# Attention of a decoder step: lone tokens in two parts by halves of the heads, one scaling of four on GpSimd, new cache rows written in a step of their own

## The chip, the cores and the metric

The kernel runs on one core of a Trainium2 chip. The core has a matrix engine (TensorE, PE in the profile; its weight loads are PEld), VectorE (DVE), ScalarE (ACT), GpSimd (POOL) and SyncE (SP), which here issues most transfers. The metric is the time of one execution on the device in microseconds (us), lower is better; "before" is the median of three runs.

## The reference, cut to what matters

One inference step of a two-layer decoder, for a prompt of 512 tokens and for 8 samples of one new token each. The change lies in the attention of the second layer. There are 16 query heads of 64 numbers in 4 groups of keys and values; each head has a sink, a logit that only enters the denominator.

```python
q = _rope((h @ w_q[j]).reshape(B, T, N_KV_HEADS, GROUP, HEAD_DIM), pos)
out = _window_attention(q, kk, vv, wb, pos0, attn_sinks[j]) @ w_o[j]
...
s = jnp.einsum('bnqkgd,bnskd->bnkgqs', q, k) * (HEAD_DIM ** -0.5)
s = jnp.where(mask[None, :, None, None], s, -jnp.inf)
m = jnp.maximum(jnp.max(s, axis=-1, keepdims=True), sink)
p = jnp.exp(s - m)
denom = jnp.sum(p, axis=-1, keepdims=True) + jnp.exp(sink - m)
return jnp.einsum('bnkgqs,bnskd->bnqkgd', p / denom, v)
```

For the prompt each block of 128 queries sees its own block and the one before it. Each of the 8 lone tokens sees 128 keys: 127 rows of its cache and its own new row.

## The kernel before, in words

Prompt and samples are columns of the same tiles: 520 columns, 512 of the prompt and 8 lone tokens. Every weight block is split into a high part (ScalarE, wh) and a low part (VectorE, wl), and a product is three matmuls (L513: high by high, high by low, low by high).

The attention stage is a list of named steps (class Steps). Each has an engine, a cost in us, a due time, the steps it must follow, and the buffers it takes and reads. A planner in the kernel plays this list through: whenever an engine is free it takes the step with the earliest due time whose predecessors are done. The resulting order is written out, engine by engine, and the engines run it in order. Costs and due times thus set only the order.

The steps are:

- q: eight query tiles t = 0 to 7, each of two heads e, two halves of 24 matmuls (L513, bank pa); then a copy, the rotation, a split, and the lone tokens' columns into the tile qz (L1188).
- 16 units t.h (tile t, half h of the prompt: two of four blocks). A unit is scores (L1203, bank pb, one buffer), four reductions on VectorE (L1220: mask and minimum, with the result in the tile sm), four exponents on ScalarE (L1238), two reciprocals, four scalings by them (L1246), two times transposes (L1254, bank pc) and copies (L1259), the product with the values (L1269), and the split of its result (L1280, L1284). Each row of sm has one column more, the sink's, which GpSimd writes (L1218) at a reduction's place; the exponent's sum takes it in. Of the scalings i = 0 to 3, numbers 0 and 2 are on VectorE, 1 and 3 on GpSimd.
- the lone tokens: scores with the cached keys kc (L1357), maximum with the sink, exponent, scaling, a transpose of the probabilities prS (L1396), a load of the cached values vc (L1368, on SP) with the new rows written into its first row by GpSimd (L1369), the product (L1408), a copy to oS (L1417) and a split into the columns that the projection reads (L1422, L1424). All heads of all samples go at once, due with unit 6.0; scores need all eight qz.
- o: the output projection, for each output tile m = 0 to 7 and each half g of the heads two column halves of 12 matmuls (L513). The first column half needs only the units of its four tiles; the second holds the lone tokens' columns too.

The cached keys are loaded and transposed before the stage, in the feed-forward part ahead of it: four loads (L1042), the new rows by GpSimd (L1043), transposes (L1052). The tiles kc and vc have four buffers together (tag S).

Of the kernel before, what the change touches and what calls it, by code (L numbers as in the profile page):

```python
# [231 lines left out]
class Steps:  # L232
# [15 lines left out]
    def order(self):  # L248
# [4 lines left out]
        while left:  # L253
# [13 lines left out]
            for n in left:  # L267
# [7 lines left out]
                for t in takes:  # L275
                    k = len(got[t]) - self.slots[t]
                    ok = ok and (k < 0 or all([passed(r, eng) for r in self.readers[t, got[t][k]]]))
# [21 lines left out]
def yoco_step(ctx, tc, ins, outs):  # L299
# [432 lines left out]
    with ff_pool() as tmp:  # L732
# [9 lines left out]
        sink_s = cp.tile([P, 4], F32, name="sink_s")  # L742
# [184 lines left out]
    with ff_pool() as tmp:  # L927
# [9 lines left out]
        for b in range(16):  # L937
            later(nc.sync.dma_start(sink_s[b * 8 : (b + 1) * 8, 0:2], attn_sinks.rearrange("l (g r) -> r (l g)", g=2)))
# [25 lines left out]
    with ff_pool() as tmp:  # L964
# [5 lines left out]
        V.tensor_scalar(sink_s[:, 2:4], sink_s[:, 0:2], -1.0, None, op0=ALU.mult)  # L970
        V.tensor_copy(sink_s[:, 0:2], sink_s[:, 2:4])
# [65 lines left out]
        def attention_prep():  # L1037


            for i in range(4):  # L1040
                kc.append(splp.tile([P, 2, 256], F32, tag="S", name="kc", bufs=4))
                later(nc.sync.dma_start(kc[i], cache_k[2 * i : 2 * i + 2].rearrange("b s g d -> s b (g d)")))  # L1042
                nc.gpsimd.dma_start(kc[i][0:1], knew[2 * i : 2 * i + 2, :])  # L1043
            yield
            for i in range(2):
                kk.append(pair(("tl", "tl"), [P, SP]))
                split(kk[i], kT[i][:, :SP])
                yield
            for i in range(4):
                pk = ps()  # L1050
                for j in range(4):
                    T.transpose(pk[:, j * P : (j + 1) * P], kc[i][:, j // 2, (j % 2) * P : (j % 2 + 1) * P], ident)  # L1052
                S.copy(kc[i].rearrange("p b c -> p (b c)"), pk)
                yield
# [9 lines left out]
    with tc.tile_pool(name="at", bufs=2) as at, tc.tile_pool(  # L1064
# [32 lines left out]
        o_due = lambda m, g: (u_due(9) + 14 + m * UP) if g == 0 else (u_due(16) + 4 + m * 2.87)  # L1097
        st = Steps(dict(a=2, b=1, c=2, w=6, rp=1, sm=6, pp=4))
# [105 lines left out]

        def least(t, h, i):
# [6 lines left out]
            if e == 0:  # L1212
                if (2 * t + h) % 3 < 2:
                    sm = at.tile([P, 2, 257], F32, tag="sm", name="sm", bufs=4)
                else:
                    sm = kvp.tile([P, 2, 257], F32, tag="kT", name="sm", bufs=2)
                vals["sm", t, h, bi] = sm
                nc.gpsimd.tensor_copy(sm[:, :, n], nsinks[:, 2 * t : 2 * t + 2])  # L1218
# [25 lines left out]
        def scale(t, h, i, eng):  # L1244
            w, den = part(t, h, i), vals["den", t, h]
            eng.tensor_scalar(w, w, den[:, i : i + 1], None, op0=ALU.mult)  # L1246
# [39 lines left out]
        for t in range(KT):  # L1286
            d = q_due(t)
            for h in range(2):
                add(
                    f"q{t}.{h}", "PE", 2.87, d + 3 * h, lambda t=t, h=h: q_part(t, h),  # L1290
# [11 lines left out]
            for h in range(2):  # L1302
# [4 lines left out]
                add("sc" + u, "PE", 0.9, d, lambda t=t, h=h: scores(t, h), after=chain("sc", f"ql{t}"), takes=("b",))  # L1307
                for i in range(4):
# [4 lines left out]
                        after=["sc" + u, "nw"] + ([f"rd{u}.{i - 1}"] if i else [f"rd{before}.3"] if n else []),  # L1313
                        takes=() if i % 2 else ("sm",), reads=[("b", "sc" + u)],
# [5 lines left out]
                for bi in range(2):  # L1320
# [5 lines left out]
                    for e in range(2):  # L1326
                        i = 2 * bi + e
                        eng, cost = ((nc.gpsimd, 0.5) if e else (V, 0.35))
                        add(
                            f"no{u}.{i}", "POOL" if e else "DVE", cost - 0.1 * small, d + 1.6 + 0.1 * i,  # L1330
# [5 lines left out]
                        takes=("c", "pp"), reads=[("sm", f"rd{u}.{2 * bi}")],  # L1336
# [12 lines left out]
        vc, sam = [], {}  # L1349
        s_due = u_due(12)  # L1350

        def s_scores():
            sam["ps"] = ps_ = bank()
            for c in range(4):
                for bq in range(4):
                    b, g = 4 * (c // 2) + bq, c % 2
                    T.matmul(  # L1357
                        ps_[32 * bq : 32 * bq + 32, c * P : (c + 1) * P],
                        qz[:, g, b - bq : b - bq + 4].rearrange("p b e i -> p (b e i)"),
                        kc[b // 2][:, b % 2, g * P : (g + 1) * P],  # L1360
# [4 lines left out]
        def s_values_load():  # L1365
            for i in range(4):
                vc.append(splp.tile([P, 2, 256], F32, tag="S", name="vc", bufs=4))
                later(nc.sync.dma_start(vc[i], cache_v[2 * i : 2 * i + 2].rearrange("b s g d -> s b (g d)")))  # L1368
                nc.gpsimd.dma_start(vc[i][0:1], vnew[2 * i : 2 * i + 2, :])  # L1369

        def s_max():
            sam["m"] = m = at.tile([P, 12], F32, name="smx", bufs=1)
            V.tensor_reduce(m[:, 0:4], sam["ps"].rearrange("p (c k) -> p c k", c=4), axis=AX.X, op=ALU.max)
            V.scalar_tensor_tensor(m[:, 0:4], m[:, 0:4], -1.0, sink_s, op0=ALU.mult, op1=ALU.min)
            V.tensor_tensor(m[:, 8:12], m[:, 0:4], sink_s, op=ALU.subtract)

        def s_exp():
            m = sam["m"]
            sam["pr"] = pr = big.tile([P, 512], F32, tag="tl", name="prS")
            for c in range(4):  # L1380
                cs_ = slice(c * P, (c + 1) * P)
                S.activation(pr[:, cs_], sam["ps"][:, cs_], AF.Exp, bias=m[:, c : c + 1], accum_out=m[:, 4 + c : 5 + c])
            S.activation(m[:, 8:12], m[:, 8:12], AF.Exp)

        def s_scale():
            m, pr = sam["m"], sam["pr"]
            V.tensor_tensor(m[:, 4:8], m[:, 4:8], m[:, 8:12], op=ALU.add)
            V.reciprocal(m[:, 4:8], m[:, 4:8])
            for c in range(4):
                cs_ = slice(c * P, (c + 1) * P)  # L1390
                V.tensor_scalar(pr[:, cs_], pr[:, cs_], m[:, 4 + c : 5 + c], None, op0=ALU.mult)

        def s_turn():
            sam["pt"] = pt = bank()
            for c in range(4):
                T.transpose(pt[:, c * P : (c + 1) * P], sam["pr"][:, c * P : (c + 1) * P], ident)  # L1396

        def s_turned():
            sam["prT"] = prT = big.tile([P, 512], F32, tag="tl", name="prT")
            S.copy(prT, sam["pt"])  # L1400

        def s_values():
            sam["po"] = po = bank()
            for b in range(NS):
                for g in range(2):
                    for e in range(2):
                        c0 = (2 * (b // 4) + g) * P + (b % 4) * 40 + e * 4
                        T.matmul(  # L1408
                            po[e * 64 : e * 64 + 64, b * 8 + g * 4 : b * 8 + g * 4 + 4],
                            vc[b // 2][:, b % 2, g * P + e * 64 : g * P + e * 64 + 64],  # L1410
                            sam["prT"][:, c0 : c0 + 4],
                            start=True,
                            stop=True,
                        )

        def s_out():
            V.tensor_copy(oS, sam["po"][:, :64].rearrange("p (b t) -> p t b", b=NS))  # L1417
# [165 lines left out]
```

## Time and profile before

| what | value |
|---|---|
| median of 3 runs | 1699.41 us (1698.33 to 1701.63) |
| profiled execution | 1699.45 us, span 1697.7 us |
| granted TensorE clock, mean | 0.985 |
| busy, share of the span | PE 97%, DVE 74%, ACT 52%, POOL 11% |
| attention stage, first query product to last projection matmul | 1153.55 to 1314.69 us |

The span is counted from the first to the last instruction. A row of a timeline gives the start, the duration, the engine, the line, the operation, what it writes and reads, and in brackets how long the engine had idled and what ended that. Rows of the view by stretches give the busy time of each engine with the number of its instructions, then the granted clock (1.00 is full speed) and the share of time in which the DMA engines worked.

### The profile page before, as it was taken

Reading aid. Unit: us, or ns where it says so; the run is one execution under the profiler, and the core shown is the slowest. Engines: PE = TensorE matmul, PEld = TensorE weight load, DVE = VectorE, ACT = ScalarE, POOL = GpSimd, SP = SyncE. Lnnn points to the kernel's source line nnn. Section 1 sums busy time; section 2 is a strip of 40 time slices with the busy share of each in tenths; the row PEclk is TensorE's granted clock in tenths of the full one; section 3 lists DMA queues with packets and bytes.
Section 4 is the critical chain, followed back from the end, with each engine's and each line's share of the span. In section 5 each row is a group of like instructions: output and inputs, shape, how many; then the busy total and the mean of one; then the engine's idle time right before and its main releaser. Section 6 shows DMA issues by size and latency. Waiting matters only on the chain.

```text
span 1697.7 us, 34520 instructions
## 1 busy us (share of the span) xinstructions
PE 1648.6 (97%) x13783; PEld 1630.4 (96%) x13783; DVE 1254.9 (74%) x2389; ACT 879.2 (52%) x1737; POOL 189.5 (11%) x245
## 2 busy tenths in 40 slices
PE   7999999999999999999999999999979999999996
PEld 6999999999899999999999999999869999999996
DVE  6875866887884885878775875888966785785765
ACT  6643643666552652655652652656754662562553
POOL 0101101000101101100201101102430110110100
PEclk9999999999999999999999999999979999999998
DMA  7646846663455655633755755652223566666631
GB/s 201 143 131 138 183 128 142 176 168 112 96 159 131 162 156 131 149 116 96 177 149 131 169 148 131 150 169 57 51 51 104 108 151 161 137 155 160 134 87 51
DMA packets 316145, 227.08 MB, mean 134 GB/s; under 512 B 9537, under 2 KB 291241, under 8 KB 315943
## 3 DMA queue, kind: packets, MB, share of 16 engines
q1 hardware_dynamic: 288176, 176.91, 37.0%
q0 software_dynamic: 23296, 41.82, 15.3%
q10 hardware_dynamic: 4510, 6.13, 1.2%
q8 instruction: 108, 1.77, 0.4%
q14 instruction: 55, 0.44, 0.1%
HBM read 180.89 MB, written 5.04 MB: 110 GB/s over the span
## 4 chain that ended last, share of the span: by engine, by line
PE 93%; DVE 3%; ACT 1%; DMA 1%; issue 1%; POOL 0%; SPq 0%; ACTq 0%; DVEq 0%; POOLq 0%
PE ps L538 47%; PE ps L513 36%; PE pa L513 5%; PE pb L1203 1%; PE ps L851 1%; PE ps L876 1%; DVE wl L193 1%; PE pc L1254 1%; PE pc L1269 1%; DVE sm L1220 0%; PE ps L477 0%; DMA raw<-in_ffn_w_gate_dram 0%; DVE acc L466 0%; DMA xt<-in_x_prompt_dram 0%; DMA vc<-in_cache_v_win_dram 0%
## 5 line engine op out<-in xcount | busy, mean ns | idle before, releaser
L192 ACT ACTIVATE wh<-raw 128x512 fp32r<-128x512 f32 (+1 forms) x710 | 429.7, 621 | 519.5 <-PE ps L513 297.8
L193 DVE TENSOR_TENSOR wl<-raw,wh 128x512 fp32r<-128x512 f32 (+1 forms) x710 | 469.0, 676 | 205.0 <-ACT wh L192 201.0
L538 PE MATMUL ps<-th,wh 128*128 128x260 f32 x1264 | 359.1, 284 | 1.6 <-ACT th L341 1.0
L538 PE MATMUL ps<-tl,wh 128*128 128x260 f32 x1264 | 359.7, 285 | 0.4 <-DVE tl L342 0.4
L538 PE MATMUL ps<-th,wl 128*128 128x260 f32 x1264 | 357.4, 284 | 1.0 <-DVE wl L193 1.0
L538 PEld LDWEIGHTS ps<-th,wh 128*128 128x128 f32 x1264 | 239.6, 190 | 2.6 <-ACT th L341 1.5
L538 PEld LDWEIGHTS ps<-tl,wh 128*128 128x128 f32 x1264 | 240.0, 190 | 0.8 <-DVE tl L342 0.8
L538 PEld LDWEIGHTS ps<-th,wl 128*128 128x128 f32 x1264 | 239.2, 190 | 1.5 <-DVE wl L193 1.5
L513 PE MATMUL ps<-hh,wh 128*128 128x260 f32 x1120 | 227.1, 284 | 0.6 <-ACT vtok L1027 0.6
L513 PE MATMUL ps<-hl,wh 128*128 128x260 f32 x1120 | 227.3, 283 | 0.0
L513 PE MATMUL ps<-hh,wl 128*128 128x260 f32 x1120 | 225.2, 283 | 0.0
L157 POOL DMA_DIRECT2D raw<-raw x79 | 68.9, 872 | 1264.5 <-DVE wl L193 488.5
L538 PE MATMUL ps<-xh,wh 128*128 128x260 f32 x708 | 198.6, 283 | 1.5 <-ACT wh L192 1.5
L538 PE MATMUL ps<-xl,wh 128*128 128x260 f32 x708 | 198.8, 283 | 0.0
L538 PE MATMUL ps<-xh,wl 128*128 128x260 f32 x708 | 194.7, 282 | 1.4 <-DVE wl L193 1.4
L513 PEld LDWEIGHTS ps<-hl,wh 128*128 128x128 f32 x1120 | 173.9, 189 | 0.0
L513 PEld LDWEIGHTS ps<-hh,wh 128*128 128x128 f32 x1120 | 172.3, 189 | 0.9 <-ACT vtok L1027 0.9
L513 PEld LDWEIGHTS ps<-hh,wl 128*128 128x128 f32 x1120 | 172.8, 189 | 0.0
L692 DVE TENSOR_TENSOR u<-ps,R 128x520 f32<-128x520 f32 x96 | 66.9, 698 | 106.3 <-PE ps L513 106.3
L538 PEld LDWEIGHTS ps<-xh,wh 128*128 128x128 f32 x708 | 133.4, 188 | 1.9 <-ACT wh L192 1.9
L538 PEld LDWEIGHTS ps<-xl,wh 128*128 128x128 f32 x708 | 133.3, 188 | 0.0
L538 PEld LDWEIGHTS ps<-xh,wl 128*128 128x128 f32 x708 | 131.4, 189 | 1.8 <-DVE wl L193 1.8
(253 smaller groups left out, 3110.9 us busy)
## 6 DMA issues: line engine op xcount, KB each, us to landing
raw<-in_ffn_w_gate_dram SPq DMA_DIRECT2D x87, 512.0 KB
raw<-in_ffn_w_up_dram SPq DMA_DIRECT2D x87, 512.0 KB
raw<-in_ffn_w_down_dram SPq DMA_DIRECT2D x32, 1024.0 KB
raw<-raw POOLq DMA_DIRECT2D x79, 256.0 KB, 3.3
S<-in_ffn_w_up_dram SPq DMA_DIRECT2D x79, 256.0 KB
S<-raw POOLq DMA_DIRECT2D x79, 256.0 KB, 4.8
raw<-in_ffn_w_down_dram SPq DMA_DIRECT2D x16, 768.0 KB
raw<-in_w_q_dram SPq DMA_DIRECT2D x8, 512.0 KB
```

The costliest lines, as they stand in the source:

```text
L157: G.dma_start(blk(raw, 2, 1), blk(raw, 1, 1), accum_op=ALU.add)
L192: nc.scalar.activation(dh, src, AF.Copy)
L193: nc.vector.tensor_tensor(dl, src, dh.bitcast(F32), op=ALU.subtract)
L513: T.matmul(banks[:, hf, :H], a[:, kk, :], hcols(b, hf), start=(first and i == 0), stop=(last and i == 2),)
L538: T.matmul(bank[:, :H], a[:, kk, :], b, start=(not more and kk == 0 and i == 0), stop=(kk == 3 and i == 2), skip_group_check=more,)
L692: V.tensor_tensor(halves(u), banks[m][:, :, :H], halves(R), op=ALU.mult)
L851: T.matmul(o, a[:, s], b[:, kk, :], start=(n == 0), stop=(n == 5))
L876: T.matmul(po[:, half * 256 : half * 256 + 256], z[:, tau, c], b, start=(i == 0), stop=(i == len(lst) - 1),)
L1203: T.matmul(o, q_[rows_, qc], k_[rows_, kc_], start=(i == 0), stop=(i == 2))
L1254: T.transpose(pt[:, o : o + P], vals["sm", t, h, bi][:, e, kt * P : (kt + 1) * P], ident)
L1269: T.matmul(po[rows_, bi * P : (bi + 1) * P], vtok[:, max(b - 1, 0) + kt, v0 : v0 + 64], vals["pp", t, h, bi][:, kt * 256 + e * P : kt * 25 ...
```

## The change

The lone tokens are done in two parts, g = 0 for the first four query tiles and g = 1 for the other four, each with its own scores, load, scaling and product; part 0 is due with unit 3.1, part 1 with unit 6.1. The tiles of cached keys and values are cut for that: one holds four samples and half of the heads (four pieces of 128 numbers for each row) instead of two samples with all heads (two pieces of 256). The probabilities have tiles of their own (prS in the pool at) and no longer use the tag tl.

Of the four scalings of a unit only number 1 stays on GpSimd; number 3 goes to ScalarE. The sink's columns are written by a step of their own, sk, one for each unit, ahead of its reductions. The new value rows are a step sn on GpSimd, and sw stands for their landing. Some costs in the list are corrected (a half of a query tile 2.87 to 3.0, a scaling on GpSimd 0.5 to 1.2), and the planner counts right when a step takes two buffers of a kind.

```diff
-                for t in takes:
-                    k = len(got[t]) - self.slots[t]
+                for i, t in enumerate(takes):
+                    k = len(got[t]) + takes[:i].count(t) - self.slots[t]
...
-                kc.append(splp.tile([P, 2, 256], F32, tag="S", name="kc", bufs=4))
-                later(nc.sync.dma_start(kc[i], cache_k[2 * i : 2 * i + 2].rearrange("b s g d -> s b (g d)")))
-                nc.gpsimd.dma_start(kc[i][0:1], knew[2 * i : 2 * i + 2, :])
+                g, j = i // 2, i % 2
+                kc.append(splp.tile([P, 4, P], F32, tag="S", name="kc", bufs=4))
+                later(nc.sync.dma_start(kc[i], cache_k[4 * j : 4 * j + 4, :, 2 * g : 2 * g + 2].rearrange("b s e d -> s b (e d)")))
+                nc.gpsimd.dma_start(kc[i][0:1], knew[4 * j : 4 * j + 4, g * P : (g + 1) * P])
...
+        S_DUE = (u_due(7), u_due(13))
...
+        def sink_cols(t, h):
+            for bi in range(2):
...
+                nc.gpsimd.tensor_copy(sm[:, :, keys(2 * h + bi)], nsinks[:, 2 * t : 2 * t + 2])
...
-            eng.tensor_scalar(w, w, den[:, i : i + 1], None, op0=ALU.mult)
+            if eng == "ACT":
+                S.activation(w, w, AF.Copy, scale=den[:, i : i + 1])
+            else:
+                (V if eng == "DVE" else nc.gpsimd).tensor_scalar(w, w, den[:, i : i + 1], None, op0=ALU.mult)
...
+                add("sk" + u, "POOL", 0.5, d - 0.1, lambda t=t, h=h: sink_cols(t, h), after=chain("sk"), takes=("sm", "sm"))
...
-                        eng, cost = ((nc.gpsimd, 0.5) if e else (V, 0.35))
+                        eng, cost = (("DVE", 0.35), ("POOL", 1.2), ("DVE", 0.35), ("ACT", 0.5))[i]
...
-                later(nc.sync.dma_start(vc[i], cache_v[2 * i : 2 * i + 2].rearrange("b s g d -> s b (g d)")))
-                nc.gpsimd.dma_start(vc[i][0:1], vnew[2 * i : 2 * i + 2, :])
+        def s_values_load(g):
+            for j in range(2):
+                vc[g, j] = splp.tile([P, 4, P], F32, tag="S", name="vc", bufs=4)
+                later(nc.sync.dma_start(vc[g, j], cache_v[4 * j : 4 * j + 4, :, 2 * g : 2 * g + 2].rearrange("b s e d -> s b (e d)")))
+
+        def s_values_new(g):
+            for j in range(2):
+                nc.gpsimd.dma_start(vc[g, j][0:1], vnew[4 * j : 4 * j + 4, g * P : (g + 1) * P])
...
-        add("ss", "PE", 1.3, s_due, s_scores, after=[f"qz{t}" for t in range(KT)], takes=("c",))
-        add("sl", "SPQ", 0.1, s_due + 0.1, s_values_load, after=["ss"])
...
-        add("s6", "PE", 2.2, s_due + 0.7, s_values, after=["s5", "sl"], takes=("c",))
+            add(
+                f"ss{g}", "PE", 0.9, d, lambda g=g: s_scores(g),
+                after=[f"qz{t}" for t in range(4 * g, 4 * g + 4)] + pre, takes=("c",),
+            )
+            sadd("sl", "SPQ", 4.5, d + 0.1, s_values_load, ["ss"])
+            sadd("sn", "POOL", 1.1, d + 0.2, s_values_new, ["sl"])
+            sadd("sw", "SWQ", 2.5, d + 0.3, None, ["sn"])
...
+            sadd("s6", "PE", 1.3, d + 0.7, s_values, ["s5", "sw"], takes=("c",))
```

What the planner makes of it stands in the order of the instructions. Three places matter.

On TensorE before, at the end of the units: pc_16446 is a unit's product with the values, sm the tiles that are transposed, prS and vc the lone tokens' probabilities and values, pa a projection's bank.

```order
L1269 MATMUL pc_16446<-pp,vtok 64x128 x8
L1254 MATMUL pc_16456<-ident,sm 128x128 x2
L1396 MATMUL pc_16471<-ident,prS 128x128 x4
L1254 MATMUL pc_16477<-ident,sm 128x128 x4
L1408 MATMUL pc_16489<-prT,vc 64x4 x32
L1269 MATMUL pc_16522<-pp,vtok 64x128 x6
L1254 MATMUL pc_16533<-ident,sm 128x128 x4
L513 MATMUL pa_16110<-th,wh 128x260 x2
```

Steps of units 6.1 to 7.1 stand one behind the other with no projection in between; the projection begins in earnest with the last row.

On TensorE now, part 0 (its scores stand ahead of the last half of the last query tile, which ends with the first row):

```order
L513 MATMUL pa_15899<-hh,wl 128x260 x2
L1263 MATMUL pc_16039<-ident,sm 128x128 x4
L1263 MATMUL pc_16047<-ident,sm 128x128 x4
L1410 MATMUL pc_16061<-ident,prS 128x128 x2
L1278 MATMUL pc_16072<-pp,vtok 64x128 x8
L1263 MATMUL pc_16087<-ident,sm 128x128 x2
L1263 MATMUL pc_16098<-ident,sm 128x128 x4
L1421 MATMUL pc_16105<-prT,vc 64x4 x16
L1207 MATMUL pb_16136<-tl,xh 128x256 x2
```

Between the last query product and part 0's values (L1421) there are transposes and one product with the values, no projection. Further on, a column half of the projection (8 rows, 12 matmuls) stands behind nearly every transpose or product; this is part 1's end:

```order
L513 MATMUL pa_16577<-th,wl 128x260
L1421 MATMUL pc_16634<-prT,vc 64x4 x16
L1263 MATMUL pc_16658<-ident,sm 128x128 x4
L1263 MATMUL pc_16666<-ident,sm 128x128 x4
L513 MATMUL pa_16673<-th,wh 128x260 x2
```

So part 1 and units 5.0 to 7.1 now alternate with projection halves of the first half of the heads.

On GpSimd before, at the new value rows (vnew); sm_16373 is the tile of TensorE's second row above, pc_16456:

```order
L1218 COPY sm_16373<-nsinks_102 128x2
L1218 COPY sm_16378<-nsinks_102 128x2
L1369 DMA vc_16388<-vnew_9961 1x2x256
L1369 DMA vc_16391<-vnew_9961 1x2x256
L1369 DMA vc_16394<-vnew_9961 1x2x256
L1369 DMA vc_16397<-vnew_9961 1x2x256
L1246 TENSOR_SCALAR sm_16373<-sm_16373,den_16372 128x128
L1218 COPY sm_16431<-nsinks_102 128x2
```

On GpSimd now, at the rows of part 0 (sm_16068 and sm_16123 are of units 5.0 and 5.1):

```order
L1255 TENSOR_SCALAR sm_15890<-sm_15890,den_15926 128x256
L1381 DMA vc_15986<-vnew_9961 1x4x128
L1381 DMA vc_15988<-vnew_9961 1x4x128
L1216 COPY sm_16068<-nsinks_102 128x2
L1216 COPY sm_16070<-nsinks_102 128x2
L1216 COPY sm_16123<-nsinks_102 128x2
L1216 COPY sm_16125<-nsinks_102 128x2
L1255 TENSOR_SCALAR sm_16068<-sm_16068,den_16085 128x128
```

Two writes stand in a row instead of four, with the columns of two units behind them, and fewer scalings in between.

155 lines of the change are left out of this document (80 added, 75 removed).

## The prediction

> **What bounds the kernel now.** I read the page first, then the chain of waits, then cut the attention stage into stretches and asked for its waits.
>
> ```profile
> PE 1648.6 (97%) x13783; PEld 1630.4 (96%) x13783; DVE 1254.9 (74%) x2389; ACT 879.2 (52%) x1737; POOL 189.5 (11%) x245
> ```
>
> TensorE is busy 97% of the span, so time can be won only where it idles or where its clock is held back. The chain of waits says where that is (start, duration, what):
>
> ```profile
> 1153.55 5.74 PE pa L513 x48
> ...
> 1217.89 2.87 PE pa L513 x24
> 1220.76 1.02 PE pc L1269 x16
> 1221.79 0.59 PE pc L1254 x4
> 1222.37 0.92 PE pb L1203 x12
> ...
> 1251.77 4.36 DMA vc<-in_cache_v_win_dram
> ...
> 1257.91 0.61 POOL sm L1246
> ...
> 1268.26 13.14 PE pa L513 x96
> ...
> 1284.31 30.38 PE pa L513 x252
> ```
>
> The attention stage runs from 1153.55 (first query product) to 1284.31 + 30.38 = 1314.69 us. Up to 1223 the chain is TensorE alone; then come a load of cached values, GpSimd, and only from 1268 TensorE again. The stage in stretches (columns: start:end, length, busy time of each engine, granted clock, DMA share, GB/s):
>
> ```profile
> core 0: us, PE busy (x) PEld busy (x) DVE busy (x) ACT busy (x) POOL busy (x), PEclk, DMA share, GB/s
> 1153.50:1160.30 6.80, 6.80 (x60) 6.80 (x59) 4.49 (x8) 3.23 (x6) 0.65 (x3) 1.00 0.41 106
> 1160.30:1170.20 9.90, 9.90 (x87) 9.63 (x88) 9.28 (x29) 3.15 (x6) 0.00 (x0) 1.00 0.20 50
> 1170.20:1223.20 53.00, 52.95 (x504) 48.34 (x504) 48.57 (x163) 39.88 (x114) 25.00 (x36) 1.00 0.24 52
> 1223.20:1249.70 26.50, 21.88 (x232) 17.38 (x234) 23.15 (x83) 19.92 (x63) 12.66 (x20) 0.97 0.19 41
> 1249.70:1268.30 18.60, 13.07 (x158) 10.96 (x157) 9.41 (x44) 9.02 (x39) 5.97 (x10) 0.68 0.19 59
> 1268.30:1284.30 16.00, 16.00 (x129) 15.69 (x128) 6.49 (x10) 4.27 (x7) 0.00 (x0) 0.89 0.25 66
> 1284.30:1314.70 30.40, 30.40 (x256) 30.40 (x255) 22.71 (x35) 15.63 (x26) 0.00 (x0) 1.00 0.37 101
> ```
>
> TensorE idles 0.05 + 4.62 + 5.53 = 10.20 us of 161.2 (length less busy time). Clock: busy time times what is missing from 1.00 gives 21.88 x 0.03 = 0.66, 13.07 x 0.32 = 4.18, 16.00 x 0.11 = 1.76, together 6.60 us. Both make 16.80 us; the work itself, at full clock, is 161.2 - 16.8 = 144.4 us. That is the ceiling of anything done to this stage's waits. Who TensorE waits for between 1223 and 1270 (total, times, longest):
>
> ```profile
> PE pc L1254 <- POOL sm L1246: 5.0, 2, 4.1
> PE pb L1203 <- DVE nm L1220: 1.6, 2, 0.8
> PE pc L1396 <- ACT pp L1259: 1.3, 1, 1.3
> PE pc L1254 <- DVE hl L1284: 1.0, 2, 0.6
> PE pc L1269 <- ACT pp L1259: 0.8, 2, 0.5
> ```
>
> Half of it is one wait of a transpose for a scaling on GpSimd. GpSimd's own timeline and the SP queue's say why (in brackets: idle before, and what ended it), with the line on the new rows' time to landing from the view of their source line:
>
> ```profile
> 1250.76 1.91 SPq L1368 DMA_DIRECT2D vc<-in_cache_v_win_dram  x4
> 1254.06 1.19 POOL L1369 DMA_DIRECT2D vc<-vnew  x2 [5.43 <-PE pc L1269]
> 1256.68 0.50 POOL L1369 DMA_DIRECT2D vc<-vnew  x1 [1.44 <-DMA vc<-in_cache_v_win_dram]
> DMA to landing us min/median/max: 1.5/2.0/3.0
> ```
>
> GpSimd stands at the writes of the new value rows, each of which must follow its tile's load, from before 1254 to 1257.9; the scaling queued behind them (1257.91 in the chain) is what the transpose needs.
>
> **The change part by part.** The sum is made against the profiled execution, 1699.45 us with a span of 1697.7, which is 0.04 us above the median of the three runs.
>
> *Lone tokens in two parts, earlier.* Part 0 needs only the first four query tiles, so it is queued behind the scores of unit 4.1, among the last query products, where TensorE did not idle (third stretch). With its result the first half of the output projection is complete in input, and its pieces (the 1.44 us halves: 30.38 us / 252 x 12) can stand between the units. Before, that material lay from 1268 on, behind everything. So units and projection overlap, and the waits of the fourth and fifth stretches get cover. TensorE's own work is the same: 32 score, 4 transpose, 64 value matmuls, now in halves; nothing added.
>
> The smaller steps, from the groups by form of the stage and one row of VectorE's timeline:
>
> ```profile
> L1246 POOL TENSOR_SCALAR sm<-sm,den 128x256 f32<-128x256 f32 x24 | 28.7, 1198 | 31.9 <-DVE den L1242 26.2 <-PE pb L1203 3.8 <-PE pc L1254 1.9
> L1246 POOL TENSOR_SCALAR sm<-sm,den 128x128 f32<-128x128 f32 x8 | 6.6, 830 | 19.9 <-DVE den L1242 19.8
> L1238 ACT ACTIVATE sm<-sm,nm 128x257 f32<-128x257 f32 x48 | 24.2, 507 | 7.0 <-POOL sm L1218 4.0 <-DVE nm L1220 2.8
> L1373 DVE TENSOR_REDUCE smx<-pc 128x4 f32<-128x512 f32 x1 | 0.7, 691 | 0.1
> L1400 ACT COPY prT<-pc 128x512 f32<-128x512 f32 x1 | 0.6, 586 | 0.2 <-PE pc L1396 0.2
> L1259 ACT COPY pp<-pc 128x256 f32<-128x256 f32 x8 | 3.0, 372 | 0.0
> 1252.33 0.16 DVE L1374 SCALAR_TENSOR_TENSOR smx<-smx,sink_s 128x4 f32<-128x4 f32 x1
> ```
>
> VectorE: the halved reduction and five small operations more, 5 x 0.16 plus at most 0.2, are 1.0 us: 125.1 us of a stage of about 148 (144.4 and the 3.5 of the sum below), 85%. ScalarE: the copy of the turned probabilities becomes two of 0.37 (+0.16), one small exponent more (at most 0.5). Neither lies on TensorE's path while products fill it.
>
> *One scaling of four on GpSimd.* The fourth scaling of each of 16 units, always 128x256, leaves GpSimd (16 x 1.198 = 19.2 us less) for ScalarE. No copy between two SBUF tiles with a column as scale is in the trace; its bounds are the 128x256 copy, 0.37, and the exponent, 0.51, a gain of 0.7 to 0.8 us in each unit's chain. I take 0.5: 8 us, so ScalarE goes from 95.1 to 104 of 148, 70%. TensorE gets nothing by that alone; it waits less for the second transpose of a unit.
>
> *Sink columns as an own step.* The 32 copies stay; they are queued ahead of the units instead of in the reductions. Cost nothing, hidden as long as GpSimd is not held; behind the new rows of part 0 stand the columns of units 5.0 and 5.1 (front part), and then the exponents wait.
>
> *New rows as an own step.* GpSimd now waits twice for two loads, not once for four. Before, from the SP queue's first issue to the first new row was 1254.06 - 1250.76 = 3.3 us; two issues take 1.19, the landing 1.5 to 3.0: 6.0 to 7.5 us. TensorE's queue has between part 0's scores and its values (front part): scores 0.92, half a query 2.87, transposes 3 x 0.59 + 0.3, values 1.02, in all 6.9 us, besides the two transposes of the probabilities. So the values of part 0 wait between 0 and 7.5 - 6.9 + 1.2 = 1.8 us (the last if a scaling of 1.2 us, the first row above, is still ahead on GpSimd); I take 0.6. Part 1 has four projection halves more in between, 5.8 us: no wait.
>
> *Cached keys in pieces of half the length* (512 B instead of 1 KB in HBM). Their load ends a wait of GpSimd, whose new row then leads to a transpose of TensorE (POOL and PE timelines, landing from the view of L1043, and two stretches of one us):
>
> ```profile
> 1131.84 0.53 POOL L1043 DMA_DIRECT2D kc<-knew  x1 [40.45 <-DMA kc<-in_cache_k_win_dram]
> DMA to landing us min/median/max: 2.0/4.5/4.9
> 1134.38 0.60 PE L1052 MATMUL ps<-ident,kc 128*128 128x128 f32 x4
> 1129.00:1130.00 1.00, 1.00 (x11) 1.00 (x10) 1.00 (x3) 0.97 (x2) 0.00 (x0) 1.00 1.11 343
> 1135.00:1136.00 1.00, 1.00 (x11) 1.00 (x11) 1.00 (x3) 0.77 (x2) 0.00 (x0) 1.00 1.16 340
> ```
>
> 1131.84 + 2.0 is 1133.84, 0.5 us before the transpose: nearly no slack. At 1129 the 1 KB pieces of the keys move beside query weights at 343 GB/s; at 1135 query weights alone, in 512 B pieces, move at 340. So the pieces cost between 0 and, if 1 MB came at two thirds of the rate, about 1.5 us of load, 1.0 on TensorE; I take 0.3. The Trainium skill speaks against this edit (Perfetto Trace Analysis, DMA Optimizations): transfers below 2 KB carry a notable overhead each, and it advises larger ones. By that rule my sum would use the upper bound, 0.7 us later; the rows, with equal rates, do not bear it out.
>
> **The sum.** Ceiling -16.8. Left over: half of the fourth stretch's hand-over gaps, 4.62 / 2 = 2.3 (bounds 0 and 4.62), since the row of transposes behind the last query product has no projection half in it; clock in them 0.3; part 0's new rows 0.6; keys 0.3. Together 3.5, a gain of 13.3: 1699.45 - 13.3 = 1686.2 us. The stage after it moves along: its weights are issued as the projection's are used up. On the clock, the Trainium skill (TensorE: Matmul & The Clock Gate, What's actually happening) says that the clock halves after an idle window of about 3.4 us. The 0.68 behind the wait of 4.1 us agrees; by that rule the short gaps that I leave would cost no clock, and the sum would be 1685.9.
>
> **The rivals.**
> (a) VectorE binds. It works 81.0 of 89.4 us from 1160.3 to 1249.7, 91%, and in the fourth stretch, with no query product to cover, TensorE loses 5.28 of 26.5 us, 20%. If that rate holds for 45 us of units despite the projection halves, 9.0 us are lost: gain 7.8, 1691.7 us. For it: VectorE's 125 us must fit into 148. Against: 91% of VectorE went with 0.05 us of idle in the third stretch.
> (b) Slower: GpSimd's wait strikes twice. Place: the two pairs of new-row writes. If at both the columns or the scaling behind them come as late as they did at 1257.9, each costs the fifth stretch's 5.53 + 4.18 and the 1.76 after it, 11.5 us; twice, with the fourth stretch's 5.28, 28.2 against 16.8 now: 1710.9 us. It decides where the loads land over 3.3 us after issue, while no projection half is queued ahead of what waits; part 0 is like that, part 1 is not.
> (c) No change: the stage ends earlier, but the start of the next waits for weights, or the projection's halves still stand behind the units: 1699.4. The order of instructions speaks against the latter, one DMA share of 0.37 in the last stretch against the former.
>
> **How the numbers follow.** Forecast 0.70, (a) 0.17, (b) 0.08, (c) 0.05. Low end: the ceiling, 1699.45 - 16.8 = 1682.6, and 0.6 for work that comes out shorter: 1682.0. High end: (a), 1692.0. A measurement of this kernel tells about 0.2%, 3.4 us, from no change; forecast and (a) are faster by more: 0.87; (c) 0.05; (b) 0.08.
>
> **What would show it.** In the profile of the changed kernel: from first query product to last projection about 148 us; idle of TensorE under 5 us in it, no stretch below 0.9 of the clock; no wait of a transpose for a GpSimd scaling above 1 us; the writes of new value rows in two pairs, part 0's values waiting under 1.8 us; the key transposes without a gap. Wrong if VectorE shows above 90% with TensorE idling over 8 us (a), or if the two GpSimd waits are on the chain (b).

## The result, and the profile after

The changed kernel takes 1685.24 us (median of 4 runs, 1681.81 to 1686.83) against 1699.71 us (4 runs, 1698.33 to 1701.63). That is 14.5 us less by the medians; the ratio is 0.9911, with an interval of 0.9893 to 0.993, which makes 15 us. The forecast was 1686.2. The profiled execution is the slowest of the four, 1686.83 us with a span of 1685.0; one execution of the same kernel differs from the next by up to 5 us, so the pieces of a profile are compared stage by stage.

Part 1 of the page shows as much work as before, and 6 us less of busy TensorE, which is the clock:

```profile
PE 1642.3 (97%) x13783; PEld 1626.2 (97%) x13783; DVE 1254.1 (74%) x2395; ACT 885.3 (53%) x1755; POOL 171.1 (10%) x229
```

The attention stage now lies between 1156.16 and 1300.83 us. The changed kernel's view by stretches, the whole stage first and then its parts (columns as before):

```profile
1156.16:1300.83 144.67, 143.78 (x1411) 133.59 (x1410) 123.38 (x376) 100.76 (x278) 25.64 (x53) 1.00 0.29 71
...
1172.80:1219.80 47.00, 47.00 (x457) 42.72 (x457) 43.84 (x156) 38.99 (x118) 12.55 (x23) 1.00 0.18 38
1219.80:1233.60 13.80, 12.91 (x154) 11.14 (x154) 13.35 (x43) 11.72 (x36) 3.83 (x7) 1.00 0.53 128
1233.60:1271.90 38.30, 38.30 (x417) 34.43 (x417) 30.80 (x109) 28.73 (x91) 8.13 (x16) 1.00 0.27 65
1271.90:1300.80 28.90, 28.90 (x242) 28.90 (x243) 21.65 (x34) 14.95 (x25) 0.00 (x0) 1.00 0.39 105
```

The stage fell from 161.14 to 144.67 us, by 16.5. TensorE idles 144.67 - 143.78 = 0.89 us in it (10.20 before), and no stretch lacks any clock. All the idle time is in the stretch of part 0, 1219.8 to 1233.6. In the next one, 38.3 us of units and projection halves, TensorE doesn't stop at all, and VectorE works 30.80 of 38.30 us, 80%. TensorE's waits in the whole stage, and the end of the chain:

```profile
PE pc L1263 <- ACT pp L1268: 0.5, 1, 0.5
PE pc L1410 <- ACT pp L1268: 0.2, 1, 0.2
```

```profile
1271.88 28.95 PE pa L513 x240
1300.83 5.76 PE ps L513 x48
```

The second fence says that the last 240 projection matmuls, 20 column halves, are a plain row, and that the first product of the next stage follows without a gap.

At part 0's new rows the wait of GpSimd is still there (4.20 us; the bracket names TensorE as what came last, not the load), but nobody waits for it. GpSimd, ScalarE and TensorE of the changed kernel:

```profile
1217.47 0.59 POOL L1216 COPY sm<-nsinks 128x2 f32<-128x2 f32 x1
1218.93 0.19 POOL L1216 COPY sm<-nsinks 128x2 f32<-128x2 f32 x1 [0.87 <-PE pc L1263]
...
1228.44 1.18 POOL L1381 DMA_DIRECT2D vc<-vnew  x2 [4.20 <-PE pa L513]
1229.62 0.80 POOL L1216 COPY sm<-nsinks 128x2 f32<-128x2 f32 x2
...
1220.57 0.51 ACT L1244 ACTIVATE sm<-sm,nm 128x257 f32<-128x257 f32 x1
...
1228.65 1.07 ACT L1268 COPY pp<-pc 128x512 f32<-128x512 f32 x2
...
1231.55 0.41 ACT L1244 ACTIVATE sm<-sm,nm 128x129 f32<-128x129 f32 x1
...
1229.29 0.44 PE L1410 MATMUL pc<-ident,prS 128*128 128x128 f32 x2 [0.24 <-ACT pp L1268]
```

Two pairs of sink's columns (L1216) matter. Those of unit 4.1 are written ahead of the rows, at 1217.47 and 1218.93, and the unit's exponents (L1244) begin at 1220.57. Those of unit 5.0 come behind the rows, at 1229.62, and the exponents that need them at 1231.55. ScalarE has begun the copies of unit 3.1's transposed tiles (L1268) before that, at 1228.65, so TensorE waits only 0.24 us for a bank. Which columns stand ahead of the rows turns out to matter below.

One thing got worse in this execution: a gap of TensorE ahead of the transposes of the keys. SP, GpSimd and TensorE of the changed kernel, and then SP before:

```profile
1126.26 5.17 SPq L1045 DMA_DIRECT2D kc<-in_cache_k_win_dram  x4
...
1133.55 0.54 POOL L1046 DMA_DIRECT2D kc<-knew  x1 [39.47 <-DMA kc<-in_cache_k_win_dram]
...
1136.96 0.63 PE L1055 MATMUL ps<-ident,kc 128*128 128x128 f32 x4 [1.26 <-DVE u L692]
```

```profile
1125.09 3.63 SPq L1042 DMA_DIRECT2D kc<-in_cache_k_win_dram  x4
```

With pieces of half the length SP takes 5.17 instead of 3.63 us to issue the four loads, and TensorE stands 1.26 us. The view names VectorE as what ended the wait; the new row, issued at 1133.55, with 3.3 us as the shortest time to landing of that line, would have landed at 1136.85, 0.1 us before the transpose. Which of the two it was is not shown.

### The profile page after: what moved, and what is told of

Read it like the earlier page. It is cut to its first block, busy times and chain, and to the rows that moved or that the text cites. A ratio compares the mean times of both kernels' runs of the same rounds, so it can differ in the third digit from the quotient of the medians.

```text
span 1685.0 us, 34510 instructions
## 1 busy us (share of the span) xinstructions
PE 1642.3 (97%) x13783; PEld 1626.2 (97%) x13783; DVE 1254.1 (74%) x2395; ACT 885.3 (53%) x1755; POOL 171.1 (10%) x229
## 4 chain that ended last, share of the span: by engine, by line
PE 93%; DVE 4%; ACT 1%; issue 1%; DMA 0%; ACTq 0%; SPq 0%; DVEq 0%
PE ps L538 47%; PE ps L513 36%; PE pa L513 5%; PE pb L1207 1%; PE ps L851 1%; PE pc L1278 1%; PE pc L1263 1%; DVE wl L193 1%; PE ps L876 1%; DVE acc L466 0%; PE ps L477 0%; DVE x L693 0%; DVE u L692 0%; PE ps L1540 0%; DMA raw<-in_ffn_w_gate_dram 0%
```

## The experiments

The prediction's theory is cover: projection products stand between the units and hide their waits. The expectations make a number of it, the projection column halves that stand ahead of the product of unit 6.1. In the kernel before there are 2. The expectations count 8 in the changed kernel; its trace has 108 projection matmuls before that product, at 1261.61 us, which are 9 halves. The rivals: GpSimd's load (two scalings a unit instead of one), the new steps by themselves, the costs in the list by themselves, and the keys. Each ratio is to runs of the kernel before on the same chip, and "gain" is what the ratio makes of 1700 us. Each fence on a stage is the view by stretches with the whole stage as one stretch; idle is length less PE's busy time, and the clock stands third from the right.

**The changed kernel again**, unedited, as the yardstick of the next three.

> The changed kernel once more, as a yardstick on this chip. If the first result stands: 1685 us (1682 to 1687), attention stage 144.7 us from first query product to last projection matmul, with under 1.5 us of TensorE idle in it, and a gap of 1.3 us ahead of the first key transpose. If the parts outside the stage differ from before only by chance, their 1.2 us before and 1.2 us behind it do not come back with the same sign and size.

1685.15 us (1682.99 to 1685.62), ratio 0.9909 (0.9896 to 0.9923). Stage 144.65 us, idle 0.88, as expected. The gap ahead of the key transposes is 2.5 us here. The stage begins at 1156.72 us, again some 3 us later than before, but behind it nothing is lost: 382.2 us to the end, against 383.0 before.

**Two scalings on GpSimd again**, all else as changed:

```diff
-                        eng, cost = (("DVE", 0.35), ("POOL", 1.2), ("DVE", 0.35), ("ACT", 0.5))[i]
+                        eng, cost = (("DVE", 0.35), ("POOL", 1.2), ("DVE", 0.35), ("POOL", 1.2))[i]
```

> The changed kernel with the fourth scaling back on GpSimd, at the corrected cost. Theory (cover by projection halves brings the gain): within 1.5 us of the changed kernel, 1685 to 1687. Rival (GpSimd's load was the cause): the transposes wait for GpSimd again, 5 us or more of the gain go, 1690 us or more.

1685.15 us, ratio 0.9918 (0.9906 to 0.9931): not to be told from the changed kernel.

```profile
1155.39:1300.97 145.58, 143.99 (x1410) 133.47 (x1410) 123.65 (x376) 94.60 (x262) 44.72 (x69) 1.00 0.29 71
```

GpSimd works 44.72 us instead of 25.64, TensorE idles 1.59 instead of 0.89. With cover, GpSimd's load costs under a microsecond.

**Both parts late**: still two parts, but both due behind unit 6.0.

```diff
-        S_DUE = (u_due(7), u_due(13))
+        S_DUE = (u_due(12), u_due(13))
```

> The changed kernel with part 0 due with unit 6.0 instead of 3.1; two parts, ScalarE's scaling and own steps stay. Theory (cover): the projection halves cannot stand between units 4.1 to 6.1, waits of 3 to 8 us return there, 1689 to 1694 us. Rival (GpSimd relieved, or new rows out of the way): as the changed kernel, 1685 to 1687.

1686.15 us (1685.06 to 1689.59), ratio 0.9921 (0.9909 to 0.9934). The theory's range missed, and the rival's holds the median. Six halves stand ahead of unit 6.1's product.

```profile
1158.39:1305.66 147.27, 143.93 (x1411) 133.40 (x1410) 123.61 (x376) 100.42 (x278) 25.78 (x53) 1.00 0.29 70
```

Idle rises to 3.34 us, so the early date is worth some 2.5 us of the stage, but ten or more of the gain stay.

**The keys later in TensorE's queue**: one more `yield` behind the loads of the cached keys, so that another piece of the feed-forward part stands ahead of the transposes.

> The changed kernel with the key transposes one output tile (4.75 us) later. Theory: the gap ahead of the first transpose is the new key row that lands late behind the pieces of half the length; it goes, the stage starts 1.3 us earlier, 1683.9 us. Rival: the gap is VectorE freeing a bank, as the view of waits names it; it then stays at the new place, and the time is that of the changed kernel, 1685.2.

1686.54 us (1682.41 to 1688.76), ratio 0.9912 (0.9898 to 0.9925). The gap is gone in the profiled execution (idle ahead of the stage from 1110 us on: 0.00, against 2.50 in the unedited run), and the time isn't better. Neither the theory's 1683.9 nor the rival's gap came.

**The scaling alone**, put into the kernel before, with 1.2 us as GpSimd's cost:

```diff
+            if eng == "ACT":
+                S.activation(w, w, AF.Copy, scale=den[:, i : i + 1])
...
-                        eng, cost = ((nc.gpsimd, 0.5) if e else (V, 0.35))
+                        eng, cost = (("DVE", 0.35), ("POOL", 1.2), ("DVE", 0.35), ("ACT", 0.5))[i]
```

> The kernel before with the fourth scaling on ScalarE and the corrected GpSimd cost, nothing else. Theory (cover): GpSimd is still held by the four new rows with a scaling behind them, and no projection half moves; between no change and a gain of 3 us, 1697 to 1700. Rival (GpSimd's load): over half of the gain, 7 us or more, 1692.5 or less.

1698.91 us (1693.42 to 1702.4), ratio 0.9986 (0.9976 to 0.9997), a gain of 2.4. The profiled execution took 1693.42 us, 5.5 below the median; its waits of TensorE in the stage:

```profile
PE pc L1272 <- ACT pp L1262: 3.2, 4, 2.0
PE pb L1203 <- DVE nm L1220: 2.6, 2, 1.8
```

No transpose waits for GpSimd any more. Other handovers take its place: products for ScalarE's copies, scores for their bank.

**The keys' layout alone** (loads, new rows and their use as in the changed kernel, the rest as before):

> The kernel before with the cached keys in pieces of half the length, nothing else. Theory: a gap of about 1.3 us ahead of the first key transpose and the stage later by as much, 1701 us. Rival (equal rates, as the rows of before had it): no gap, 1699.7.

1700.95 us, ratio 1.0006 (0.9998 to 1.0015): no change that can be told. A gap of 2.6 us stands ahead of the first key transpose, and the stage keeps its old wait:

```profile
PE pc L1255 <- POOL sm L1247: 4.9, 2, 4.0
```

**The new value rows as an own step alone** (sn, and sw for the landing, in the kernel before):

```diff
-        add("sl", "SPQ", 0.1, s_due + 0.1, s_values_load, after=["ss"])
+        add("sl", "SPQ", 5.5, s_due + 0.1, s_values_load, after=["ss"])
+        add("sn", "POOL", 2.2, s_due + 0.2, s_values_new, after=["sl"])
+        add("sw", "SWQ", 2.5, s_due + 0.3, None, after=["sn"])
```

> The kernel before with the four new value rows as a step of their own behind their loads, planned as such, nothing else; still one part, late. Theory: the longest wait, 4.1 us, and the clock it costs, about 6 us, go in part; waits for the values and hand-overs of the units stay, since nothing covers them: a gain of 3 to 8 us, 1692 to 1697. Rival (the new rows' place is the whole effect): the gain of the changed kernel, 1685 to 1687. Second rival (another wait takes its place at once): no change, 1699 to 1700.

1698.63 us, ratio 0.9994 (0.9985 to 1.0002): nothing, as the second rival had it. In the profiled execution, which took 1703.84 us:

```profile
PE pc L1254 <- POOL sm L1246: 2.5, 2, 1.6
PE pb L1203 <- DVE nm L1220: 1.9, 3, 0.9
PE pc L1399 <- DVE prS L1394: 1.7, 1, 1.7
```

The wait of 4.1 us for a scaling became one of 1.6, and 1.7 us for the lone tokens' own chain came in. Two projection halves stand ahead of unit 6.1's product, as before, so there is little to cover these waits.

**The costs alone**: the kernel before, with 3.0 us for half a query tile and 1.2 (0.83 for a small one) for a scaling on GpSimd. No instruction is added or removed; only the order moves. Six projection halves then stand ahead of unit 6.1's product instead of two.

```diff
-                    f"q{t}.{h}", "PE", 2.87, d + 3 * h, lambda t=t, h=h: q_part(t, h),
+                    f"q{t}.{h}", "PE", 3.0, d + 3 * h, lambda t=t, h=h: q_part(t, h),
...
-                        eng, cost = ((nc.gpsimd, 0.5) if e else (V, 0.35))
+                        eng, cost = ((nc.gpsimd, 1.2) if e else (V, 0.35))
```

> The kernel before with three numbers of the planner corrected (a half of a query tile 3.0, a scaling on GpSimd 1.2, its short form 0.83) and no other change: one part, two scalings on GpSimd, columns and new rows as before. In its order six projection halves stand ahead of unit 6.1's product, where the kernel before has two and the changed one eight. Theory (what counts is how many halves stand there, whatever brought them): most of the gain, 8 us or more, 1686 to 1692. First rival (the two parts are the cause): under 3 us, 1697 to 1700. Second rival (GpSimd's load or its blocked queue is the cause): no gain, 1698 to 1701.

1692.64 us (1691.69 to 1693.39), ratio 0.9951 (0.9939 to 0.9963): 8.3 us, half of the gain, by numbers in a list. The theory's 8 us came, though the time lies 0.6 us outside its range.

```profile
1156.08:1309.46 153.38, 147.30 (x1411) 137.33 (x1410) 123.48 (x370) 94.31 (x260) 43.73 (x69) 0.97 0.27 67
```

**One part**: the changed kernel with its steps, costs and scaling, but all lone tokens at once, due with unit 6.0, and the old layout. Two halves stand ahead of unit 6.1's product, as before.

```diff
-        S_DUE = (u_due(7), u_due(13))
+        s_due = u_due(12)
...
+        add("ss", "PE", 1.3, s_due, s_scores, after=[f"qz{t}" for t in range(KT)], takes=("c",))
+        add("sl", "SPQ", 5.5, s_due + 0.1, s_values_load, after=["ss"])
+        add("sn", "POOL", 2.2, s_due + 0.2, s_values_new, after=["sl"])
+        add("sw", "SWQ", 2.5, s_due + 0.3, None, after=["sn"])
```

> The changed kernel with the lone tokens in one part again, due with unit 6.0, keys in the old layout; the scaling on ScalarE, the columns' and the new rows' own steps and the corrected costs stay. Two projection halves stand ahead of unit 6.1's product. Theory (halves): a small gain, 0 to 4 us, 1696 to 1700. First rival (two parts): the same. Second rival (GpSimd relieved): most of the gain, 1685 to 1690.

1691.5 us (1689.79 to 1693.11), ratio 0.9944 (0.9932 to 0.9956). By the theory almost nothing should have been gained with two halves; 9.5 us were, of which the corrected costs that this kernel holds give 8.3 alone. The theory that the count of halves is all has fallen. The rival that GpSimd's relief is all (1685 to 1690) falls short by 1.5 us too.

```profile
1155.13:1305.37 150.24, 143.57 (x1411) 133.10 (x1410) 123.20 (x370) 100.11 (x276) 25.20 (x53) 1.00 0.28 69
```

```profile
PE pb L1203 <- DVE nm L1222: 2.5, 3, 1.9
PE pc L1274 <- ACT pp L1264: 1.6, 4, 0.6
PE pc L1363 <- DVE qz L1188: 1.2, 1, 1.2
```

What is left here is 6.67 us of idle time in many short handovers, with the clock at 1.00. The long wait behind GpSimd is not among them.

**Two parts alone**: the changed kernel with its layout, its parts and its dates, but with the rest undone (columns in the reductions, rows written with the load, old costs, two scalings on GpSimd). Eight halves stand ahead of unit 6.1's product, one fewer than in the changed kernel.

> The changed kernel with everything but the two parts and their layout undone: two scalings on GpSimd at the old costs, columns written in the reductions, new rows issued with their loads. Eight halves ahead of unit 6.1's product. Theory (halves) and first rival (two parts): most of the gain, 9 us or more, 1685 to 1690. Second rival (GpSimd): nothing or little, 1695 to 1700, with transposes waiting for scalings behind the new rows.

1692.72 us (1686.43 to 1695.07), ratio 0.9945 (0.9928 to 0.9962). Its halves are there, and the gain is 9.4 us of 15. The profiled execution took 1686.43 us, 6 below the median, but its stage is 6.2 us longer than the changed kernel's. One wait of TensorE holds most of that:

```profile
1152.80:1303.62 150.82, 145.43 (x1411) 135.18 (x1410) 124.89 (x376) 95.22 (x262) 45.18 (x69) 0.98 0.28 69
```

```profile
PE pc L1404 <- ACT pp L1266: 4.3, 1, 4.3
```

**Both late, two scalings on GpSimd**: the two edits that each cost next to nothing, together in the changed kernel.

> The changed kernel with both parts late and two scalings on GpSimd at the corrected cost; each of the two alone cost 0 to 1 us. Six halves ahead of unit 6.1's product. Theory (halves): within 4 us of the changed kernel, 1685 to 1689. Second rival (early part and ScalarE's scaling are two covers for one wait on GpSimd, either enough): with both gone the wait is back, 1692 or more.

1689.73 us (1687.34 to 1696.42), ratio 0.9941 (0.9924 to 0.9958). Both ranges missed. Together the two edits cost some 5 us, more than the sum of the two alone. The rival's reason isn't borne out: no transpose waits for GpSimd. TensorE idles 3.91 us in short pieces, and the rest is clock (146.79 us of busy time against 143.78). Seven halves stand ahead of unit 6.1's product, not the six of the expectation.

```profile
1155.09:1305.79 150.70, 146.79 (x1410) 135.74 (x1410) 124.44 (x376) 94.54 (x262) 43.86 (x69) 0.98 0.28 68
```

**Two parts and the costs**, the last run: the previous "two parts alone" with the corrected costs. It differs from "two scalings on GpSimd" only by the missing own steps for columns and rows. Its order has ten halves ahead of unit 6.1's product, more than any other.

```diff
-                    f"q{t}.{h}", "PE", 2.87, d + 3 * h, lambda t=t, h=h: q_part(t, h),
+                    f"q{t}.{h}", "PE", 3.0, d + 3 * h, lambda t=t, h=h: q_part(t, h),
...
-                        eng, cost = (("DVE", 0.35), ("POOL", 0.5), ("DVE", 0.35), ("POOL", 0.5))[i]
+                        eng, cost = (("DVE", 0.35), ("POOL", 1.2), ("DVE", 0.35), ("POOL", 1.2))[i]
```

> The changed kernel without its own steps for sink columns and new value rows, and with two scalings on GpSimd; kept are the two parts, the layout of the cached rows and the corrected costs (half a query tile 3.0, scaling on GpSimd 1.2). Against the run with two parts and old costs (0.9945) this adds the costs alone; against the run with two scalings on GpSimd (0.9918) it lacks the own steps alone. Its order has ten projection halves ahead of unit 6.1's product. Theory that the order is all (halves between the units, set by parts and costs): 1684 to 1688 us, ratio 0.991 to 0.993, idle of TensorE in the stage under 2.5 us. Rival, that the own steps are needed, since GpSimd's new rows otherwise stand ahead of columns that the planner counts as written: 1690 to 1695, ratio 0.9945 to 0.9975, and one wait of TensorE of 3 to 5 us whose chain leads over ScalarE's exponents to GpSimd's new rows of part 0, as the 4.3 us were with the old costs.

1692.0 us (1689.03 to 1694.89), ratio 0.9956 (0.9942 to 0.9969). The rival was right, with its number: the one wait is 3.66 us. The chain of waits of this kernel, from the issue of part 0's load on, and below it ScalarE and TensorE with their idle time:

```profile
1223.27 5.80 DMA vc<-in_cache_v_win_dram
...
1229.64 0.26 POOL vc L1375
...
1230.88 0.21 POOL sm L1222
...
1231.12 1.09 ACT sm L1242 x4
1232.21 0.48 ACT pp L1266
...
1232.73 0.69 PE pc L1404 x2
```

```profile
1231.12 0.51 ACT L1242 ACTIVATE sm<-sm,nm 128x257 f32<-128x257 f32 x1 [5.31 <-POOL sm L1222]
...
1232.12 1.05 ACT L1266 COPY pp<-pc 128x512 f32<-128x512 f32 x2
...
1232.73 0.69 PE L1404 MATMUL pc<-ident,prS 128*128 128x128 f32 x2 [3.66 <-ACT pp L1266]
```

The load lands at 1229.07 (1223.27 + 5.80). GpSimd writes the rows, then a sink's column (L1222, 1230.88). ScalarE has stood 5.31 us at the exponents for that column, and the copies of the transposed tiles stand behind the exponents; TensorE wants the bank that they empty. GpSimd's own rows show which column it is:

```profile
1221.84 0.18 POOL L1222 COPY sm<-nsinks 128x2 f32<-128x2 f32 x1
1229.64 0.56 POOL L1375 DMA_DIRECT2D vc<-vnew  x1 [7.62 <-PE pb L1207]
...
1230.88 0.20 POOL L1222 COPY sm<-nsinks 128x2 f32<-128x2 f32 x1
```

By the planner's order it is the second column of unit 4.1; the first was written ahead of the rows, at 1221.84. The unit's last two exponents wait for it, and the copies behind them are those of unit 3.1. In the changed kernel the exponents of unit 4.1 stand ahead of these copies too, but both of the unit's columns stand ahead of the rows, so they don't wait for them. In "two scalings on GpSimd", which has the own steps, the unit's columns are written at 1219.90 and 1221.27 and the rows at 1229.96. The wait of 4.3 us in "two parts alone" has the same form with a column of unit 5.0: rows from 1227.31, two scalings, the column at 1230.54, and ScalarE 3.81 us idle for it.

Undoing the own steps lengthens the stage from 145.58 to 150.92 us:

```profile
1156.24:1307.16 150.92, 147.26 (x1410) 137.59 (x1410) 123.66 (x376) 94.31 (x262) 44.75 (x69) 0.97 0.29 69
```

Why the orders differ is read from the list, not measured. Without own steps the columns are written inside the reductions and the rows inside the load, which costs 0.1 us in the list. Neither occupies GpSimd in the planner's account: the rows are queued as soon as the load is issued, and what is queued behind them counts as done when it is not. With sk the columns are queued ahead of the unit's reductions, and with sn the rows stand behind a load of 4.5 us. Both steps were undone together, so which of the two does it is not shown.

The runs side by side (halves: ahead of unit 6.1's product; idle: TensorE's in the stage; steps: sk and sn/sw; late: both parts due behind unit 6.0):

| kernel | two parts | steps | costs | scalings on GpSimd | halves | idle, us | ratio |
|---|---|---|---|---|---|---|---|
| before | no | no | no | 2 | 2 | 10.20 | 1 |
| the scaling alone | no | no | scaling | 1 | 2 | 7.55 | 0.9986 |
| the costs alone | no | no | yes | 2 | 6 | 6.08 | 0.9951 |
| one part | no | yes | yes | 1 | 2 | 6.67 | 0.9944 |
| two parts alone | yes | no | no | 2 | 8 | 5.39 | 0.9945 |
| two parts and the costs | yes | no | yes | 2 | 10 | 3.66 | 0.9956 |
| both late, two scalings | late | yes | yes | 2 | 7 | 3.91 | 0.9941 |
| both late | late | yes | yes | 1 | 6 | 3.34 | 0.9921 |
| two scalings on GpSimd | yes | yes | yes | 2 | 9 | 1.59 | 0.9918 |
| changed | yes | yes | yes | 1 | 9 | 0.88 | 0.9909 |

Two parts without the steps, or the steps without two parts, stop at 0.9944 to 0.9956: each leaves one stall in place, a single wait of about 4 us behind GpSimd's new rows and the clock after it in the one case, 6 us of short handovers in the other. Both are needed for the last 6 us. A sum of single effects doesn't exist here.

## Why the prediction was right, point by point

The time and the bulk of its working hold; the cause was told too simply. That 1686.2 came within a microsecond is in part luck: the own steps and the corrected costs were put at nothing, and the gaps left over were put too high.

- **The ceiling** (idle time and missing clock of the stage, 16.8 us) was the right frame. The stage gave 161.14 - 144.67 = 16.5 us. The allowance for work that comes out shorter was used: TensorE's 143.78 us are 0.6 below the 144.4 counted.
- **Left-over gaps** were the term sized wrongly: 2.3 us of handover, 0.3 of clock and 0.6 for part 0's rows stood in the sum, 3.2 together. Measured are 0.89 us of idle time and no lost clock, so the stage took 144.67 us instead of about 148. Part 0's values wait for nothing: from the issue of two loads at 1224.06 to the first new row (1228.44) it took 4.4 us, the two writes 1.18 and the landing 1.5, about 7.1 in all where 6.0 to 7.5 were forecast, and the values come at 1232.49.
- **Cover**, the step "units and projection overlap", with the waits covered by it, is true as far as it goes, but it isn't the whole cause. With ten halves between the units and no own steps, 3.66 us of wait and some 3.5 us of clock remained (147.26 us of busy time at 0.97, against 143.78).
- **The own steps** stood in the sum at nothing or at a cost. This step failed: they are worth some 6 us beside the two parts, a ratio of 0.9956 against 0.9918. The prediction named the kind of wait (columns of units 5.0 and 5.1 behind part 0's rows, "and then the exponents wait") as a danger of the own step. The runs show the reverse: without the steps it is a column of unit 4.1 or 5.0 that stands behind the rows and stops ScalarE for 5.31 or 3.81 us and TensorE for 3.66 or 4.3; with them TensorE has no wait above 0.9 us there.
- **The corrected costs** got no term at all. In the kernel before they alone bring 8.3 us; added to the two parts alone they bring nothing (0.9945 and 0.9956).
- **The scaling**: "TensorE gets nothing by that alone" holds within 2.4 us alone, and within a microsecond in the changed kernel. Its 0.5 us on ScalarE measured 508 ns, the upper of the two bounds; ScalarE came to 100.76 us (104 forecast), VectorE to 123.38 (125.1).
- **The keys** were put at 0.3 us. The profiled execution shows a gap of 1.26 at them; alone the layout costs between nothing and 0.15%, 2.6 us. But the gap is not tied to it: in the old layout the profiled executions show 0 to 2.6 us at the same transposes (2.6 with only the rows' step), in the new one 0.2 to 3.4 where the transposes stand at the same place. What makes it come and go stays open.
- **Outside the stage** nothing was forecast. In the profiled execution 2.6 us were lost ahead of it and 1.2 behind it; they are why 16.5 us in the stage became 12.7 in that span. The 1.2 did not come back. The 2.6 did, as 3.2 in the second profile of the changed kernel, but they are not tied to the change either: kernels with the code of before ahead of the stage began it at 1155.13 to 1159.72 us, and 1153.55 is early among them.
- **Rival (a)**, VectorE: did not bind, though it works 43.84 of 47.00 us, 93%, from 1172.8 to 1219.8; TensorE has no idle time there. **Rival (b)** did not come as priced, but its mechanism is real: in the two kernels with parts and without steps GpSimd's rows held TensorE once, through ScalarE, for 4.3 and 3.7 us. **Rival (c)** fell: 20 column halves stand behind the units now, and the next stage follows them without a gap.

On the clock, the prediction set the Trainium skill (TensorE: Matmul & The Clock Gate, What's actually happening: the clock halves after an idle window of about 3.4 us) beside the trace. The runs agree only in part. "One part" has no wait above 1.9 us and a clock of 1.00, as the rule has it. "Both late, two scalings" has no wait above 0.9 us either, and yet (its stretches around unit 6.0):

```profile
1240.00:1250.00 10.00, 7.00 (x96) 5.05 (x92) 9.48 (x40) 8.15 (x33) 5.28 (x9) 1.00 0.19 54
1250.00:1260.00 10.00, 10.00 (x98) 9.03 (x96) 5.99 (x24) 5.43 (x21) 2.84 (x4) 0.66 0.20 55
```

Three microseconds of idle time in short pieces were followed by a stretch of ten at 0.66. The kernel with the keys later has the changed kernel's order in the stage. Here is one stretch of it, and the same stretch of the changed kernel again, with nearly the same busy time of TensorE:

```profile
1230.00:1240.00 10.00, 9.35 (x103) 7.90 (x104) 9.45 (x36) 7.50 (x27) 2.23 (x8) 0.83 0.49 107
```

```profile
1230.00:1240.00 10.00, 9.36 (x116) 8.01 (x116) 9.87 (x39) 8.86 (x31) 4.01 (x9) 1.00 0.50 107
```

One lost clock and the other did not. Here the measurement decides: gaps well under 3.4 us can be followed by a lower clock, though not in every execution, and the prediction was right to leave a term for it. What decides it stays open.

## What to carry to other kernels

Where a planner or a hand-written list sets the order, give every instruction that can make its engine wait a step of its own with its true time. Here GpSimd stood 7.62 us ahead of a write that follows a load, the column queued behind it stopped ScalarE for 5.31 us, and ScalarE's queue stopped TensorE for 3.66. Try the costs in the list first: three numbers got half of this gain in the old kernel, though nothing beside the two parts alone. And take single edits out of the finished kernel as well as putting them into the old one: the own step for the rows gained nothing in the old kernel, and the own steps for rows and columns are worth over 6 us in the new one.

## What was not expected of the hardware

- Issuing the four loads of cached keys with 512 B pieces took SP 4.86 to 6.05 us in nine profiled executions, against 3.63 to 4.31 in five with 1 KB pieces, for the same bytes.
- The same kernel's executions spread over 3 to 9 us (1682.99 to 1685.62; 1693.42 to 1702.4) with one and the same order of instructions, and two kernels with the same code ahead of the stage (before, and the new rows' step alone) reached it at 1153.55 and 1159.72 us. A single profile can therefore show a gap of 1 to 3 us that its median doesn't have.
